# Two attention branches of a hybrid decoder kernel: probabilities divided before their transpose, outputs formed feature-major in column halves, and a new job order

## The chip, the cores and the metric

One Trainium2 chip, one core. The metric is the device time of one execution in microseconds; lower is better. The kernel was run three times before the change, and one further execution was profiled. All times below are microseconds (us) unless marked ns.

The engines are named as the profile names them: PE is TensorE (matrix products and transposes), PEld its weight loads, DVE is VectorE, ACT is ScalarE, POOL is GpSimd, and SPq is the queue of SyncE, which issues every DMA of this kernel in program order.

## The reference, cut to what matters

Two layers over a sequence of 512 tokens of width 1024. Each layer normalises x, projects it once to 9668 columns, runs five branches on parts of these columns, projects every branch output back to 1024 channels under a sigmoid gate, sums the five, applies an output projection, normalises and adds to x. The change touches two of the branches:

```python
def dsa_branch(c, pos):          # sparse attention, 4 heads x 64
    ...                          # a relu indexer picks up to 128 keys per query
    logits = jnp.einsum('bqhd,bqnhd->bhqn', qb, k_sel) * HEAD_DIM ** -0.5
    p = jax.nn.softmax(jnp.where(valid, logits, -1e30), -1)
    out = jnp.einsum('bhqn,bqnhd->bqhd', p, v_sel)
    ...
    return out * jax.nn.silu(g.astype(jnp.float32))

def memory_branch(c, mem_kv):    # cross attention into 256 memory tokens, 4 heads x 64
    ...
    p = jax.nn.softmax(jnp.einsum('bshd,bmhd->bhsm', q, km) * HEAD_DIM ** -0.5, -1)
    o = jnp.einsum('bhsm,bmhd->bshd', p, vm).reshape(bsz, seq, XATT_W)
    return o * jax.nn.silu(g.astype(jnp.float32))

def reference(...):
    for l in range(DEPTH):       # DEPTH = 2
        cols = jnp.einsum('bsd,dn->bsn', rms_norm(x, norm_pre[l]), w_in[l])
        ...
        ys = (rwkv7_branch(...), dsa_branch(...), retention_branch(...), s5_branch(...), memory_branch(...))
        for i in range(N_BRANCH):   # merged += gate_i * (ys[i] @ w_branch[l, i])
            ...
        x = x + rms_norm(merged @ w_out[l], norm_post[l])
    return x
```

## The kernel before, in words

**Dense work.** The large products (input projection, gates, branch projections, output projection) use weights split into two parts, `wh` and `wl`. A 128x512 piece of weight is fetched into one of five `raw` buffers, ACT casts it to `wh`, DVE forms `wl = raw - wh`, and PE runs three products for every 128 contraction rows (`mm3`). Each such piece of work is a `Job`. Jobs carry needs (flags of things that must be ready), and the strings `ORDER[0]` and `ORDER[1]` give the priority of the jobs in each layer: `select` takes the first one in the list whose needs are met and whose buffers fit. The letters are projections (`rsg`, `w`, `xq`, ...), and `g0` to `g4` are the gate and branch-projection jobs of the five branches: 0 is RWKV, 1 is the sparse attention, 2 retention, 3 S5, 4 cross attention. A gate job of branch b needs the branch output `y{l}{b}`.

**Branches.** Each branch is a generator (`Lane`) that yields after each step. `run` interleaves lanes with the dense work while the instructions are written out. It keeps its own estimate of each engine's clock (`Sched`); a lane's next step is written when its inputs should be ready at the PE's clock, except when DVE or ACT is more than `LAG` ahead of PE. The engines then execute their queues strictly in that written order. `LANES` gives the priority of the lanes, and `idx>4` means that lane `idx` waits for `y{l}4`. At most six lanes are active. The lane `tab` builds the tables of the S5 branch, on POOL mostly; all gate jobs of a layer need it.

**The two attention branches.** `branch_x` handles 128 queries at a time in four blocks. Scores of heads are formed in row halves of the array (`score_pair`: 64 contraction rows each, two heads side by side). DVE takes the maxima, ACT the exponentials `pr` with their sums `dn`, DVE the reciprocal. PE transposes the probabilities, ACT copies them to `xpT`, and PE forms

```python
T.matmul(po[:, h, :], pT[p][:, j, m, :], vm[:, m, 64 * h:64 * h + 64], start=m == 0, stop=m == 1)
```

so the stationary operand is 128x128 probabilities and 64 value columns move past it. The output has tokens on partitions. DVE multiplies by `1/dn` while it evicts to `xon`, and after the fourth block `to_fm` transposes the whole output back to features on partitions (eight transposes per branch and layer). `branch_dsa` does the same with causal blocks of 128 to 512 keys: one product per head and key block, `pv_(h - 1)` written behind the transposes of head h. Its tiles are `dsc` (scores, then probabilities), `dpT`, `dv` (values) and `don`.

**The seam between layers.** `finish_out` adds the normalised output of one 128-token tile to x and at once goes on to `put_hT`, which takes the squares on ACT (`xn<-x`), the scale, and the transposes into the next layer's `hh` and `hl`. The first jobs of every layer are `rq` and `rk` on halves of the tokens, so that they can start when the first two tiles are done.

Of the kernel before, what the change touches and what calls it, by code (L numbers as in the profile page):

```python
# [20 lines left out]
S = 512  # L21
# [13 lines left out]
LAG = 11.5  # L35
# [4 lines left out]
ORDER = ("rsg rv w wg g0 xq xsg di su dsg ssg dq g4 g2 dk mem1 dv g3 mem g1",  # L40
         "xsg dq g0 w di rsg wg g4 su dsg ssg dk dv g3 g1 g2")
LANES = ("ret idx>4 s5>4 ms1>3 rwkv dsa ms0 tab x>2", "idx>4 dsa>0 tab ret x rwkv>t s5")
# [40 lines left out]
class Sched:  # L83
# [5 lines left out]
    def __init__(self):  # L89
# [6 lines left out]
        self.last = (128, False, True)  # L96
# [24 lines left out]
    def matmul(self, t, ready, name, lhs, rhs):  # L121
# [11 lines left out]
        lk, lmove, lr = self.last  # L133
        if (lk, lmove) != (k, move) and self.share == 1.0:
            t += 0.085 if r and (lmove or not lr) else 0.09 if lk != k else 0.0
        self.last = (k, move, r)
# [86 lines left out]
def hybrid_kernel(ctx: ExitStack, tc: tile.TileContext, x, mem, positions, norm_pre, norm_post, norm_mem, w_in,  # L223
# [57 lines left out]
    x0 = [load_x(0, 0)]  # L281
    ncst = COFF["qdec"][0]
# [5 lines left out]
    npre = {0: bcast_row(norm_pre[0], "npre")}  # L288
# [492 lines left out]

    def rope_swap(raw, n):
# [89 lines left out]
    def branch_x(l):  # L872
# [5 lines left out]
        on = sb("xon", [128, 4, 256])  # L878
        for i in range(4):
# [14 lines left out]
            V.reciprocal(dn, dn)  # L894
            yield
# [10 lines left out]
            po = psb((128, 4, 64))  # L906
            for p in range(2):
                for j in range(2):
                    h = 2 * j + p
                    for m in range(2):  # L910
                        T.matmul(po[:, h, :], pT[p][:, j, m, :], vm[:, m, 64 * h:64 * h + 64],
                                 start=m == 0, stop=m == 1)
            V.tensor_tensor(on[:, i, :].rearrange("t (j p e) -> t j p e", j=2, p=2),
                            po.rearrange("t (j p) e -> t j p e", p=2),
                            dn.rearrange("t (p j) -> t j p", p=2)[:, :, :, None].to_broadcast([128, 2, 2, 64]),
                            op=OP.mult)
# [4 lines left out]
        for j in range(2):  # L921
            ps = to_fm(on, j)
            V.tensor_tensor(ys[l, 4][:, j, :], ps, sg[:, j, :], op=OP.mult)
            yield
# [119 lines left out]
    def branch_dsa(l):  # L1044
# [11 lines left out]
        on = sb("don", [128, 4, 256])  # L1056
        for i in range(4):
# [16 lines left out]
            V.reciprocal(dn, dn)  # L1074
            yield
            po = psb((128, 4, 64))
            pTs = []

            def pv_(h):
# [3 lines left out]
            for h in range(4):  # L1083
# [6 lines left out]
                if h:  # L1090
                    pv_(h - 1)
# [338 lines left out]
    def s5_tables(l):  # L1430
# [41 lines left out]
        for r_, w in enumerate((s5_b_re, s5_b_im)):  # L1472
            bv = w[l].rearrange("(b q) p c -> q p b c", q=2)
            for q in range(2):
                SY.dma_start(Bt[64 * q:64 * q + 64, r_], bv[q])
# [518 lines left out]
```

## Time and profile before

| | |
|---|---|
| median of three runs | 1432.06 us (1430.72 to 1433.5) |
| the profiled execution: its time | 1431.76 us |
| the profiled execution: span from first to last instruction | 1430.0 us |
| PE busy | 1373.7 us (96%) |
| DVE busy | 950.2 us (66%) |
| ACT busy | 558.3 us (39%) |
| POOL busy | 279.1 us (20%) |
| mean granted TensorE clock | 0.986 |

The time of an execution is the span plus 1.8 us around it. Busy shares are of the span. A matrix product in fp32 appears as two records in the trace, a transpose as one; the durations of single PE records overlap, so the spacing of their starts is what they cost.

### The profile page before, as it was taken

The page shows a single profiled execution, that of the slowest core. Times are in us where ns is not written, and L with a number is a line of the kernel's source. Part 1 is how long each engine was busy: PE and PEld are TensorE (multiplying, and loading weights), DVE is VectorE, ACT ScalarE, POOL GpSimd, SP SyncE. Part 2 cuts the span into 40 slices and gives each one's busy share as a digit, 9 for nine tenths or more (in the row PEclk, how much of TensorE's full clock was granted, in tenths as well). Part 3 has the DMA queues.
Part 4 walks back from the last instruction along what each step waited for, and adds up shares of the span by engine and source line. Part 5 has one row for each costly group of instructions (what it writes and reads, how often), then busy time and mean ns, then how long its engine had stood idle before and what let it go on. Part 6 is the DMA issues. An engine that isn't in the chain of part 4 may idle for free.

```text
span 1430.0 us, 21718 instructions
## 1 busy us (share of the span) xinstructions
PE 1373.7 (96%) x7774; PEld 1147.8 (80%) x7774; DVE 950.2 (66%) x2027; ACT 558.3 (39%) x1196; POOL 279.1 (20%) x329
## 2 busy tenths in 40 slices
PE   5999999999999999999979899999999999999997
PEld 5878777788878887888979788687888788778887
DVE  5677565978867864444666567668788786844465
ACT  5433445333334235233554452443323332344353
POOL 0194241000111111110019523210010112411000
PEclk9999899999999999999999899999999999999999
DMA  6644425364242432344656624263534322422355
GB/s 193 176 114 127 122 89 141 89 184 126 72 121 74 129 101 52 89 118 125 188 152 177 180 78 134 60 143 94 141 103 147 89 67 72 114 67 81 99 163 181
DMA packets 243414, 170.60 MB, mean 119 GB/s; under 512 B 27657, under 2 KB 228331, under 8 KB 243307
## 3 DMA queue, kind: packets, MB, share of 16 engines
q1 hardware_dynamic: 243307, 169.22, 42.6%
q8 instruction: 61, 1.00, 0.3%
q14 instruction: 46, 0.38, 0.1%
HBM read 144.53 MB, written 18.87 MB: 114 GB/s over the span
## 4 chain that ended last, share of the span: by engine, by line
PE 82%; DVE 6%; POOL 4%; DMA 3%; ACT 2%; issue 2%; SPq 1%; POOLq 0%; DVEq 0%; ACTq 0%
PE d L209 62%; PE b L209 19%; DVE wl L209 2%; POOL sar L209 2%; DMA raw<-in_w_out_dram 1%; POOL sta L209 1%; DMA raw<-in_w_in_dram 1%; DVE x L209 1%; SPq L209 1%; ACT wh L209 0%; DMA posi<-in_positions_dram 0%; DMA x<-in_x_dram 0%; DMA rsw<-rq 0%; POOL sem L209 0%; POOL rsw L209 0%
## 5 line engine op out<-in xcount | busy, mean ns | idle before, releaser
L209 PE MATMUL d<-hh,wh 128*128 128x512 f32 (+2 forms) x1232 | 488.3, 396 | 13.5 <-ACT wh L209 13.5
L209 PE MATMUL d<-hh,wl 128*128 128x512 f32 (+2 forms) x1232 | 474.3, 385 | 6.6 <-DVE wl L209 6.5
L209 PE MATMUL d<-hl,wh 128*128 128x512 f32 (+2 forms) x1232 | 472.1, 383 | 0.0
L209 DVE TENSOR_TENSOR wl<-raw,wh 128x512 fp32r<-128x512 f32 x448 | 334.0, 761 | 139.2 <-ACT wh L209 135.6
L209 ACT CAST wh<-raw 128x512 fp32r<-128x512 f32 x448 | 268.7, 617 | 165.6 <-PE d L209 111.9
L209 PEld LDWEIGHTS d<-hh,wh 128*128 128x128 f32 (+1 forms) x1232 | 235.6, 191 | 73.1 <-issue 15.0
L209 PEld LDWEIGHTS d<-hh,wl 128*128 128x128 f32 (+1 forms) x1232 | 234.8, 191 | 58.4 <-DVE wl L209 10.1
L209 PEld LDWEIGHTS d<-hl,wh 128*128 128x128 f32 (+1 forms) x1232 | 235.8, 191 | 42.3 <-issue 0.5
L209 POOL TENSOR_TENSOR mg<-mg,gth 128x512 f32<-128x512 f32 x48 | 69.9, 1457 | 486.2 <-DVE gth L209 486.2
L209 DVE SCALAR_TENSOR_TENSOR gth<-gth,d 128x512 f32<-128x512 f32 x64 | 43.9, 686 | 107.2 <-PE d L209 103.4
L209 ACT ACTIVATE gth<-d 128x512 f32<-128x512 f32 (+1 forms) x90 | 51.9, 577 | 159.7 <-PE d L209 155.0
L209 PE MATMUL b<-wh,mgs 128*128 128x256 f32 x320 | 63.2, 283 | 5.6 <-ACT wh L209 4.1
L209 PE MATMUL d<-yl,wh 128*128 128x512 f32 x160 | 62.9, 393 | 0.7 <-DVE yl L209 0.7
L209 PE MATMUL d<-yh,wl 128*128 128x512 f32 x160 | 62.8, 393 | 0.0
L209 PE MATMUL d<-yh,wh 128*128 128x512 f32 x160 | 62.7, 392 | 0.0
L209 PEld LDWEIGHTS b<-wh,mgs 128*128 128x128 f32 x320 | 52.1, 190 | 6.3 <-ACT wh L209 4.3
L209 DVE MAX8 dm<-dac 128x8 f32<-128x256 f32 (+2 forms) x96 | 52.8, 550 | 0.1
L209 DVE MATCH_REPLACE8 dac<-dm,dac 128x256 f32<-128x256 f32 (+2 forms) x96 | 52.1, 543 | 0.0
L209 PE MATMUL b<-wl,mgs 128*128 128x256 f32 x160 | 45.5, 285 | 0.3 <-DVE wl L209 0.3
L209 POOL TENSOR_TENSOR ors<-ors,mhalf 128x1 f32<-128x1 f32 x8 | 5.0, 634 | 203.3 <-DVE ors L209 203.3
L209 PE MATMUL d<-wh,mgs 128*128 128x256 f32 x192 | 40.6, 285 | 2.0 <-DVE ou L209 2.0
L209 POOL TENSOR_TENSOR rsw<-rsw,sinT 128x1024 f32<-128x1024 f32 (+1 forms) x12 | 29.7, 2480 | 44.0 <-DMA rsw<-diq 20.7
(399 smaller groups left out, 2067.9 us busy)
## 6 DMA issues: line engine op xcount, KB each, us to landing
raw<-in_w_in_dram SPq DMA_DIRECT2D x324, 256.0 KB, 3.4
raw<-in_w_out_dram SPq DMA_DIRECT2D x64, 256.0 KB, 4.7
raw<-in_w_branch_dram SPq DMA_DIRECT2D x40, 256.0 KB, 3.2
x<-in_x_dram SPq DMA_DIRECT2D x8, 512.0 KB, 6.0
raw<-in_w_mem_kv_dram SPq DMA_DIRECT2D x16, 256.0 KB, 2.9
s5tab<-sar SPq DMA_DIRECT2D x8, 256.0 KB, 2.0
s5Wi<-sar SPq DMA_DIRECT2D x4, 512.0 KB
nn<-wNt SPq DMA_DIRECT2D x8, 256.0 KB
```

What stands on the lines that cost most here:

```text
L209: r = f(*args, **kw)
```

## The change

Four things change.

1. In both attention branches the probabilities are multiplied by `1/dn` on DVE before they are transposed. The products swap operands: the stationary operand is now 64 value columns, the transposed probabilities move (128 columns), and two heads are written into the two column halves of the array by a new helper, `value_pair`. The outputs land with features on partitions, ACT copies them to `on`, and `to_fm` with its eight transposes per branch and layer is gone. In the sparse attention the first pair of heads is multiplied behind the transposes of the third head, the second pair after a yield.
2. `ORDER`, `LANES` and `LAG` have new values, and the planner's PE model counts a change of the array's column part as well.
3. At the start the load of `npre` comes ahead of the constants and of the second x tile, and the first weights are split before the transposes of the second x tile.
4. Three places get a `yield`: behind the stores of the S5 tables, before each load of `sBt`, and between the addition to x and `put_hT` in `finish_out`.

```diff
-LAG = 11.5
+LAG = 10.5
-ORDER = ("rsg rv w wg g0 xq xsg di su dsg ssg dq g4 g2 dk mem1 dv g3 mem g1",
-         "xsg dq g0 w di rsg wg g4 su dsg ssg dk dv g3 g1 g2")
-LANES = ("ret idx>4 s5>4 ms1>3 rwkv dsa ms0 tab x>2", "idx>4 dsa>0 tab ret x rwkv>t s5")
+ORDER = ("xq rsg rv w g1 wg g3 xsg dsg di ssg su g4 dk dq dv mem1 mem g2 g0",
+         "w xsg g1 dq di rsg dv g0 ssg su g3 g4 wg dk g2 dsg")
+LANES = ("ms1>3 tab ms0 s5 dsa>2 ret x rwkv idx>4", "ret s5>2 rwkv>4 x tab dsa>0 idx>2")
...
     x0 = [load_x(0, 0)]
+    npre = {0: bcast_row(norm_pre[0], "npre")}
...
     x0.append(load_x(0, 1))
-    npre = {0: bcast_row(norm_pre[0], "npre")}
...
+    def value_pair(out, v, pT, first, last):
+
+        sched.share = 0.5
+        for p in range(2):
+            T.matmul(out[halves[p]], v[:, halves[p]], pT(p), start=first, stop=last, skip_group_check=True)
+        sched.share = 1.0
...
# branch_x
-        on = sb("xon", [128, 4, 256])
+        on = sb("xon", [128, 2, S])
...
             V.reciprocal(dn, dn)
+            V.tensor_tensor(pr, pr, dn[:, :, None].to_broadcast([128, 4, NMEM]), op=OP.mult)
...
-            po = psb((128, 4, 64))
-            for p in range(2):
-                for j in range(2):
-                    h = 2 * j + p
-                    for m in range(2):
-                        T.matmul(po[:, h, :], pT[p][:, j, m, :], vm[:, m, 64 * h:64 * h + 64],
-                                 start=m == 0, stop=m == 1)
-            V.tensor_tensor(on[:, i, :]..., po..., dn..., op=OP.mult)
+            po = psb((128, 2, 128))
+            for j in range(2):
+                for m in range(2):
+                    value_pair(po[:, j, :], vm[:, m, 128 * j:128 * j + 128], lambda p: pT[p][:, j, m, :],
+                               m == 0, m == 1)
+            A.copy(on[:, :, ts], po)
...
         for j in range(2):
-            ps = to_fm(on, j)
-            V.tensor_tensor(ys[l, 4][:, j, :], ps, sg[:, j, :], op=OP.mult)
-            yield
+            V.tensor_tensor(ys[l, 4][:, j, :], on[:, j, :], sg[:, j, :], op=OP.mult)
+        yield
...
# branch_dsa
             V.reciprocal(dn, dn)
-            yield
-            po = psb((128, 4, 64))
+            for h in range(4):
+                V.tensor_scalar(sc[h], sc[h], dn[:, h:h + 1], None, op0=OP.mult)
+            yield
+            po = psb((128, 2, 128))
...
-            def pv_(h):
+            def pv_(j):
                 for m in range(i + 1):
-                    T.matmul(po[:, h, :], pTs[h][:, 128 * m:128 * m + 128], v[:, m, 64 * h:64 * h + 64],
-                             start=m == 0, stop=m == i)
+                    value_pair(po[:, j, :], v[:, m, 128 * j:128 * j + 128],
+                               lambda p: pTs[2 * j + p][:, 128 * m:128 * m + 128], m == 0, m == i)
...
-                if h:
-                    pv_(h - 1)
+                if h == 2:
+                    pv_(0)
             yield
-            pv_(3)
-            V.tensor_tensor(on[:, i, :]..., po, dn..., op=OP.mult)
+            pv_(1)
+            A.copy(on[:, :, ts], po)
...
# s5_tables
                 SY.dma_start(s5d["tab"][2 * l + b][:, r_], ...)
+            yield
...
             for q in range(2):
+                yield
                 SY.dma_start(Bt[64 * q:64 * q + 64, r_], bv[q])
...
# finish_out
         if l < L - 1:
+            yield
             yield from put_hT(l + 1, i, xi)
...
# first_h
-        yield from put_hT(0, i, x0[i])
+        for n, _ in enumerate(put_hT(0, i, x0[i])):
+            if n == 1 and i == 1:
+                prefetch(0, 0)
+            yield
```

## Rows read from the trace of the kernel before

**Rows 1.** The page, busy time, share of the span and instructions.

```profile
PE 1373.7 (96%) x7774; PEld 1147.8 (80%) x7774; DVE 950.2 (66%) x2027; ACT 558.3 (39%) x1196; POOL 279.1 (20%) x329
```

**Rows 2.** Stretches of 50 us: length, busy PE, PEld, DVE, ACT, POOL, clock, DMA, GB/s.

```profile
0.00:50.00 50.00, 33.52 (x221) 31.69 (x222) 30.21 (x70) 25.45 (x47) 2.51 (x10) 0.93 0.63 180
...
300.00:350.00 50.00, 50.00 (x293) 40.86 (x292) 40.34 (x101) 16.58 (x36) 1.62 (x2) 1.00 0.44 126
...
700.00:750.00 50.00, 41.14 (x330) 40.34 (x330) 33.79 (x70) 26.54 (x64) 5.59 (x12) 0.97 0.60 179
750.00:800.00 50.00, 41.42 (x311) 40.78 (x311) 26.94 (x34) 20.56 (x43) 38.41 (x78) 0.86 0.68 189
...
1400.00:1430.00 30.00, 20.41 (x171) 19.98 (x169) 16.54 (x33) 9.57 (x23) 2.69 (x4) 0.94 0.49 164
```

**Rows 3.** The waits of PE, whole run: us in total, times, longest.

```profile
PE d L209 <- ACT wh L209: 13.5, 4, 8.4
...
PE b L209 <- ACT wh L209: 4.1, 1, 4.1
...
PE b L209 <- ACT dpT L209: 1.9, 8, 0.2
```

**Rows 4.** Group of PE instructions by form: records, busy us, mean ns.

```profile
L209 PE MATMUL b<-dv,dpT 128*128 128x64 f32 x160 | 22.5, 272 | 2.2 <-ACT dpT L209 1.9
```

**Rows 5.** Timeline, one block's value products of cross attention: start, us, what.

```profile
191.14 1.97 PEld L209 LDWEIGHTS b<-xvm,xpT 128*128 128x128 f32 x16
...
191.36 1.89 PE L209 MATMUL b<-xvm,xpT 128*128 128x64 f32 x16
```

**Rows 6.** Timeline of PE around one block's scores in row halves.

```profile
523.60 0.39 PE L209 MATMUL d<-hl,wh 128*128 128x512 f32 x1
523.83 0.40 PE L209 MATMUL d<-hh,wl 128*128 128x512 f32 x1
524.16 0.71 PE L209 MATMUL b<-dk,dq 64*128 64x128 f32 x8
...
525.14 0.39 PE L209 MATMUL d<-hl,wh 128*128 128x512 f32 x1
```

**Rows 7.** Timeline of PE from value products of sparse attention back to dense.

```profile
544.39 0.66 PE L209 MATMUL b<-dv,dpT 128*128 128x64 f32 x4
...
545.17 0.39 PE L209 MATMUL d<-hl,wh 128*128 128x512 f32 x1
```

**Rows 8.** Timeline of PE around four transposes of `to_fm`.

```profile
237.08 0.60 PE L209 MATMUL b<-cst,xon 128*128 128x128 f32 x4
...
237.75 0.39 PE L209 MATMUL d<-hl,wh 128*128 128x512 f32 x1
```

**Rows 9.** Groups of DVE instructions by form: busy, mean ns, idle before them.

```profile
L209 DVE TENSOR_TENSOR xon<-b,xdn 128x256 f32<-128x256 f32 x8 | 3.4, 419 | 6.2 <-PE b L209 6.1
...
L209 DVE TENSOR_TENSOR diq<-diq,cosT 128x1024 f32<-128x1024 f32 x2 | 2.4, 1210 | 0.0
...
L209 DVE TENSOR_SCALAR wta<-wta,hka,oka 128x512 f32<-128x512 f32 x4 | 2.2, 545 | 0.1
```

**Rows 10.** Timeline of DVE at the start of the run.

```profile
9.11 2.74 DVE L209 SCALAR_TENSOR_TENSOR xn<-x,xrs,npre 128x512 f32<-128x512 f32 x4
```

**Rows 11.** Timeline of ACT at the seam between the layers.

```profile
717.44 1.06 ACT L209 ACTIVATE xn<-x 128x1024 f32<-128x1024 f32 x1 [1.54 <-DVE x L209]
...
718.49 2.16 ACT L209 CAST wh<-raw 128x512 fp32r<-128x512 f32 x4
```

**Rows 12.** Timeline of PE 30 us later at the seam; idle time before in brackets.

```profile
749.73 0.39 PE L209 MATMUL d<-hh,wh 128*128 128x256 f32 x1 [2.99 <-ACT wh L209]
```

**Rows 13.** Timeline of the DMA queue at the S5 tables of layer 1.

```profile
779.86 5.05 SPq L209 DMA_DIRECT2D s5tab<-sar  x4
...
787.81 2.66 SPq L209 DMA_DIRECT2D raw<-in_w_in_dram  x5
```

**Rows 14.** Timeline of ACT where the last gate of layer 1 begins.

```profile
1317.69 0.62 ACT L209 CAST yh<-ys 128x512 fp32r<-128x512 f32 x1 [0.20 <-PE d L209]
```

More of the change, by code (lines that the diff above doesn't have):

```diff
@@ L95, in __init__ @@
         self.landing = [0.0] * 8
-        self.last = (128, False, True)
+        self.last = ((True, True), False, True)
         self.window, self.activity, self.half = 8.0, 0.0, True
@@ L132, in matmul @@
         t = max(t, ready)
[L133 to L136, printed above, removed]
+        part = (k > 64, c > 64)
+        last, lmove, lr = self.last
+        if (last, lmove) != (part, move) and self.share == 1.0:
+            t += 0.085 if r and (lmove or not lr) else 0.09 if last != part else 0.0
+        self.last = (part, move, r)
         self.turn(t)
@@ L905, in branch_x @@
             yield
-            po = psb((128, 4, 64))
-            for p in range(2):
-                for j in range(2):
-                    h = 2 * j + p
-                    for m in range(2):
-                        T.matmul(po[:, h, :], pT[p][:, j, m, :], vm[:, m, 64 * h:64 * h + 64],
-                                 start=m == 0, stop=m == 1)
[L913 to L916, printed above, removed]
+            po = psb((128, 2, 128))
[4 more added lines that the diff above has]
+            A.copy(on[:, :, ts], po)
         resize(f"y{l}4", c4=3)
@@ L1055, in branch_dsa @@
         v = ST[l, "dv"]
-        on = sb("don", [128, 4, 256])
+        on = sb("don", [128, 2, S])
         for i in range(4):
@@ L1089, in branch_dsa @@
                 pTs.append(pT)
-                if h:
-                    pv_(h - 1)
+                if h == 2:
+                    pv_(0)
             yield
-            pv_(3)
-            V.tensor_tensor(on[:, i, :].rearrange("t (h e) -> t h e", h=4), po,
-                            dn[:, :, None].to_broadcast([128, 4, 64]), op=OP.mult)
+            pv_(1)
+            A.copy(on[:, :, ts], po)
         resize(f"y{l}1", c4=3)
@@ L1100, in branch_dsa @@
         for j in range(2):
-            ps = to_fm(on, j)
-            V.tensor_tensor(ys[l, 1][:, j, :], ps, sg[:, j, :], op=OP.mult)
-            yield
+            V.tensor_tensor(ys[l, 1][:, j, :], on[:, j, :], sg[:, j, :], op=OP.mult)
+        yield
     def wsb(name, shape, dt=F32, bufs=2):
```

## The prediction

> **What bounds the kernel now.** I read the page's busy shares first: PE is busy for 1373.7 of 1430.0 us, so 56.3 us are idle in all [rows 1]. Then I asked for busy time in stretches of 50 us, because a share over the whole run hides where the idle time lies. It lies in three places [rows 2]: the first 50 us (16.5 idle), the seam between the layers from 700 to 800 us (8.9 and 8.6), and the last 30 us (9.6). Those make 43.5 us; the other 1250 us hold only 12.8. In the middle, as from 300 to 350 us, PE is busy all the time while DVE has 9.7 of 50 us free. So in the middle of a layer a us of PE work saved is a us of run time, as long as the lanes deliver their branch outputs in time; at the ends the time goes by what PE waits for. The waits of PE name these: `wh`, the cast weights, leads with 13.5 and 4.1 us, all at the seam, and the probabilities of the sparse attention cost only 1.9 us in eight waits [rows 3].
>
> **The change part by part.** The sum is made against the profiled execution: 1430.0 us of span and 1.8 around it make 1431.8, which is 0.3 below the median of the three runs. A change of 0.2% (2.9 us) is about what the three runs can tell from none.
>
> *Value products.* The code has 64 of them in the cross attention (2 layers, 4 blocks, 4 heads, 2 key blocks) and 80 in the sparse one, and the trace shows two records for each, 160 for the sparse one [rows 4] and 16 in each of the eight blocks of the cross attention [rows 5]. Sixteen take 1.89 us; less the 0.27 us tail of the last one that is 15 steps of 0.108 us [rows 5]. The count stays at 288 after the change, but each now streams 128 columns past 64 stationary ones. No row shows column halves. The bounds: four transposes, which stream 128 columns, take 0.67 us together with one dense record of 0.23, so 0.11 each [rows 8]; without any sharing nothing is gained. The nearest row with two products side by side is the score pair, also fp32 and also 128 moving columns: eight records in 0.71 us, less a tail of 0.30, are 7 steps of 0.059 [rows 6]. It is nearest in data type, columns and pairing, so I take 0.059: 288 x 0.049 = 14.1 us gained (0 to 15.6, the latter at half of 0.108).
>
> The Trainium skill's page "TensorEngine Tiling (Array Packing)", section "Overview" ("Theoretical Speedup"), gives up to twice the throughput when the stationary operand has at most 64 columns; by it alone this term would be 15.6, and no run here shows it yet.
>
> *Transposes.* `to_fm` goes from both branches: 8 transposes x 2 branches x 2 layers = 32, at 0.11 us [rows 8], 3.5 us gained. They enter and leave at no visible cost.
>
> *Changing the array's shape.* From a dense record to a score pair it takes 0.33 us instead of 0.23, so 0.10 to enter; from the pair to the second dense record behind it 0.98 us, less 8 x 0.059 and 0.23, so 0.28 to leave [rows 6]. Leaving the present value products costs 0.78 - 4 x 0.108 - 0.23 = 0.12 [rows 7]. The new code enters column halves 8 times in the cross attention and 16 in the sparse one: 24 x (0.10 + 0.28 - 0.12) = 6.2 us lost (0 if the halves of columns need no change of shape, 9.1 if nothing is to be deducted).
>
> *The copies of probabilities.* PE now waits once per block for the copy of head h while it has the transposes of head h+1 to do [rows 3]. Later it does three heads' transposes and then needs the copies of two. The copies run on ACT one behind the other, so the one wait gets longer by part of a copy; I take 0.25 us x 8 = 2 us lost (0 to 4).
>
> *Vector work.* The division adds 8 multiplies of 128x1024, 1.21 us each, and 32 of up to 128x512, at most 0.545 each: 9.7 and at most 17.4 us. Sixteen evictions of 0.42 us leave DVE for ACT [rows 9], where a copy of the same size should cost about the same. DVE gains at most 20 us on its 950, and ACT 7 on 558. I cost it at nothing, because the dense products of PE run beside it and DVE has 9.7 of 50 us free in a full stretch of the middle [rows 2]. Without that cover each block's chain from reciprocal to transpose would be 1.2 to 2.2 us longer, at most 27 us over 16 blocks. The new ACT copy waits for PE, as the DVE eviction does now (6.1 us in 8 cases in the cross attention [rows 9]). Behind it in ACT's queue stand casts of `wh`, and PE waits for those; but two pieces of weight are kept split ahead of PE, some 5.6 us of dense work in the middle of a layer (24 records at 0.23), and such a wait is 0.8 us. Again nothing.
>
> *The start.* DVE begins to scale the first x tile at 9.11 us, when `npre` has landed as the fourth load [rows 10]. Second in the queue, `npre` comes two loads earlier and the first tile is scaled early, but the second x tile now lands last and has squares and scale still before it. I see 1.2 us (0 to 2).
>
> *The yields.* At the seam the squares of two tiles stand in ACT's queue ahead of the cast of `wh` and wait for DVE's addition to x; the cast starts at 718.49 [rows 11], and PE stands for 4.1 us behind it; the same pattern 30 us later costs 3.0 [rows 12]. Another 8.4 us is the longest wait of the run for `wh` [rows 3]. With a yield between the addition and the squares, casts can be written in between. That longest wait comes from the DMA queue: the stores of the S5 tables sit at its head from 779.86 us until POOL has finished, four `sBt` loads follow, and the next weights go out at 787.81 [rows 13]. The yield there can take only the `sBt` part away, 2.9 us (779.86 + 5.05 to 787.81). Together 4.1 + 3.0 + 2.9 = 10 us at the most; since weights must still arrive and POOL is as late as ever, I take half, 5 us (0 to 10).
>
> *The order.* No row shows it. The middle stretches leave it 12.8 us to gain at best. I put it at zero; what it may lose is a rival.
>
> Sum: 1431.8 - 14.1 - 3.5 + 6.2 + 2 - 1.2 - 5 = 1416.2 us. All bounds on the good side give 1431.8 - 15.6 - 3.5 - 2 - 10 = 1400.7, on the bad side 1431.8 - 3.5 + 9.1 + 4 = 1441.4.
>
> **The rivals.**
>
> *The halves do not share the array.* Then the value products keep 0.108 us and the changes of shape are still paid: 1416.2 + 14.1 = 1430.3, no change. For it speaks that the two moving streams come from the same 128 partitions, unlike those of a score pair; against it, that a dense record passes 512 columns in 0.23 us, 0.45 ns each [rows 6], while a transpose needs 0.11 us for 128, 0.86 ns each [rows 8]: the moving side can deliver fp32 words at twice the rate at which such a record takes them.
>
> *Weight loads of one half do not run beside products of the other.* A record would pay 0.054 us for 64 weight columns (half of the 0.108 that 128 take now) and 0.11 for the stream, 0.164 in place of 0.059: 288 x 0.105 = 30.2 us lost, 1446.4. Rows speak against it: the 16 loads of a block take 1.97 us and its 16 products 1.89, over the same time and the same 128 rows [rows 5]. The Trainium skill's page "TensorE: Matmul & The Clock Gate", section "Part 3: Packing small matmuls — row/col tiling", says that a weight load overlaps products in flight only where their row groups differ, which would bring this about; the trace does not agree, with 0.108 us a record where load and stream in turn would take longer.
>
> *The sparse attention of layer 1 comes late.* This one is slower. Its output is cast at 1317.69 us, when the fourth gate's products are just done [rows 14], so PE has no other work left: the chain RWKV, then sparse attention, already ends on the beat. If PE saves time ahead of it and the chain does not move, the gain is lost to waiting; if the new order, in which RWKV waits for the cross attention in layer 1, makes it later, the run is longer by as much. The run ends 1431.8 - 1317.7 = 114.1 us after that cast, so it is slower than before from the point at which the cast comes after 1317.7. A chain that is late by 20 us at RWKV and by at most 8.7 at four blocks of division (4 heads x 0.545 x 4), less 15 that the PE saves ahead of it, gives 1445.5. Against it: `w` now stands first in layer 1, ahead of `xsg` and `dq`, so RWKV gets its inputs four tiles (some 22 us at 24 records of 0.23) sooner.
>
> *The order also closes gaps.* All of the yields and half of the middle gaps: 1416.2 - 5 - 6.4 = 1404.8.
>
> **How the numbers follow.** Forecast 0.58 (its own range 1409 to 1424), order closes gaps 0.14, halves do not share 0.11, loads do not overlap 0.03, late chain 0.14. The likeliest gives 1416.2. The range runs from 1401, the good bounds, to 1438, which leaves out the worst of the two slower rivals, some 2 in 10 with what may lie below 1401. Faster by over 0.2%: 0.58 + 0.14 and half of the 0.11, 0.77. Within 0.2%: 0.07, most of it from halves that do not share. Slower: 0.16.
>
> **What would show it.** In the profile after: value products with 64 stationary columns in steps of about 0.06 us; if 0.11, the halves do not share. The group of `to_fm` transposes of `xon` and `don` gone. The first dense record behind a value pair 0.2 to 0.3 us late. No ACT square between two casts of `wh` at the seam while PE waits; the wait of 8.4 us down to about 6. The last gate's cast of layer 1 some 15 us before 1317.7, with no PE idle ahead of it. The prediction is wrong if PE idle time in the middle grows beyond 12.8 us, which would be the order, or if the seam keeps its 17.5 us.

## The result and the profile after

The changed kernel takes 1415.04 us (median; 1413.4 to 1415.91) beside 1431.39 for the kernel before on the same chip: ratio 0.9889 (95% interval 0.9862 to 0.9917), 15.9 us faster by that ratio. The forecast was 1416.2. The profiled execution took 1413.4 with a span of 1411.6, again 1.8 around it. Line L209 of before is L210 here.

The page of the changed kernel, busy time [rows 1]:

```profile
PE 1357.6 (96%) x7742; PEld 1123.6 (80%) x7742; DVE 960.2 (68%) x2046; ACT 562.0 (40%) x1212; POOL 290.0 (21%) x334
```

PE is busy 16.1 us less, and its idle time is 54.0 us in place of 56.3. It lies elsewhere, as the stretches of the changed kernel show (columns as in [rows 2]):

```profile
0.00:50.00 50.00, 35.02 (x240) 32.71 (x241) 31.55 (x70) 26.88 (x50) 3.01 (x10) 0.97 0.69 191
150.00:200.00 50.00, 43.48 (x246) 35.30 (x245) 30.96 (x66) 26.66 (x68) 18.17 (x14) 0.86 0.39 119
200.00:250.00 50.00, 43.68 (x263) 32.99 (x262) 29.02 (x47) 21.96 (x59) 7.48 (x8) 0.93 0.35 88
...
700.00:750.00 50.00, 44.62 (x368) 43.57 (x367) 37.98 (x81) 29.36 (x70) 14.74 (x29) 1.00 0.67 198
750.00:800.00 50.00, 48.27 (x353) 45.39 (x352) 32.04 (x41) 24.83 (x52) 30.96 (x53) 0.97 0.84 221
```

The same view of the kernel before, for the two stretches that were not shown:

```profile
150.00:200.00 50.00, 47.45 (x243) 36.98 (x241) 31.69 (x65) 23.67 (x58) 12.30 (x9) 0.90 0.36 106
200.00:250.00 50.00, 49.33 (x278) 39.36 (x279) 27.13 (x54) 27.58 (x72) 14.09 (x13) 0.97 0.47 130
```

The seam went from 17.4 to 7.1 us idle, and its clock from 0.97 and 0.86 to 1.00 and 0.97. From 150 to 250 us, where the cross attention of layer 0 runs beside the preparation of RWKV, a hole opened: 12.8 us idle where there were 3.2, and a lower clock. The waits of PE in the changed kernel, whole run [rows 3]:

```profile
PE d L210 <- DVE wl L210: 12.6, 15, 1.6
...
PE b L210 <- DVE wrks L210: 3.7, 1, 3.7
PE d L210 <- ACT wh L210: 2.8, 2, 1.5
...
PE b L210 <- ACT dpT L210: 0.5, 1, 0.5
```

Cast weights `wh` cost 17.6 us before and cost 4.1 now (2.8 and one of 1.3). Waits for `wl`, which VectorE makes, cost 13.6 us now (12.6 and one of 1.0) where they cost 7.6. The value products by form, and one pair of the sparse attention among dense records on PE's timeline, both of the changed kernel [rows 4, 7]:

```profile
L210 PE MATMUL b<-dpT,dv 128*64 128x128 f32 x160 | 14.5, 285 | 0.8 <-ACT dpT L210 0.5
L210 PE MATMUL b<-xpT,xvm 128*64 128x128 f32 x128 | 9.4, 285 | 0.3 <-ACT xpT L210 0.3
```

```profile
1296.79 0.39 PE L210 MATMUL d<-hh,wl 128*128 128x512 f32 x1
1297.11 1.09 PE L210 MATMUL b<-dpT,dv 128*64 128x128 f32 x16
1298.13 0.50 PE L210 MATMUL d<-hh,wh 128*128 128x512 f32 x1
1298.47 0.39 PE L210 MATMUL d<-hl,wh 128*128 128x512 f32 x1
```

Sixteen records in 1.09 us, less the tail of 0.27, are 15 steps of 0.055 on the average (0.108 before). Entering takes 0.32 instead of 0.23, so 0.09; leaving 1.36 - 16 x 0.055 - 0.23 = 0.25.

The next table splits the profiled execution of each kernel, which can lie some us off the median beside it, into three stretches. The marks are the first record of each layer's output projection (its other operand is `mgs`) on PE's timeline. The seam lies in the middle stretch. The kernels e1 to e12 are told of below.

| kernel | median us | ratio to before (95%) | start to projection 0 | projection 0 to 1 | from there to the end of the span |
|---|---|---|---|---|---|
| before | 1431.39 | | 682.7 | 691.0 | 56.3 |
| changed | 1415.04 | 0.9889 (0.9862, 0.9917) | 683.5 | 671.9 | 56.2 |
| e8, yields alone | 1420.81 | 0.9946 (0.9924, 0.9967) | 684.3 | 679.0 | 56.3 |
| e3, all but the attention | 1414.83 | 0.9902 (0.9878, 0.9925) | 678.8 | 675.6 | 59.3 |
| e9, cross attention old | 1405.57 | 0.9840 (0.9818, 0.9862) | 676.0 | 671.9 | 55.9 |
| e11, sparse attention old | 1428.41 | 0.9992 (0.9974, 1.0010) | 688.3 | 683.4 | 55.7 |
| e2, attention alone | 1433.79 | 1.0040 (1.0021, 1.0059) | 681.0 | 693.7 | 55.5 |
| e5, no yields | 1429.12 | 0.9998 (0.9987, 1.0010) | 681.6 | 688.5 | 55.7 |
| e4, old order | 1417.43 | 0.9915 (0.9895, 0.9936) | 681.7 | 678.9 | 56.0 |
| e1, halves in turn | 1417.56 | 0.9912 (0.9893, 0.9931) | 684.5 | 674.0 | 57.8 |
| e6, no division | 1398.95 | 0.9793 (0.9774, 0.9812) | 673.9 | 670.1 | 55.8 |
| e7, wide products | 1421.97 | 0.9945 (0.9929, 0.9962) | 688.6 | 677.6 | 55.8 |
| e10, division on ScalarE | 1415.15 | 0.9905 (0.9886, 0.9924) | 680.3 | 677.0 | 55.7 |
| e12, division in two steps | 1414.04 | 0.9891 (0.9869, 0.9912) | 680.3 | 677.1 | 55.9 |

Differences between kernels below are those of ratios times 1430 us. The interval of a single ratio is 1.6 to 3.9 us to either side, widest for the changed kernel, so a difference of two kernels is uncertain by 4 to 5 us.

### The profile page after: what moved, and what is told of

Same layout as the page of the kernel before. It is cut to its first block, busy times and chain, and to the rows that moved or that the text cites. A ratio compares the mean times of both kernels' runs of the same rounds, so it can differ in the third digit from the quotient of the medians.

```text
span 1411.6 us, 21674 instructions
## 1 busy us (share of the span) xinstructions
PE 1357.6 (96%) x7742; PEld 1123.6 (80%) x7742; DVE 960.2 (68%) x2046; ACT 562.0 (40%) x1212; POOL 290.0 (21%) x334
## 4 chain that ended last, share of the span: by engine, by line
PE 79%; DVE 9%; DMA 3%; ACT 3%; issue 3%; POOL 3%; SPq 1%; DVEq 0%; POOLq 0%; ACTq 0%
PE d L210 62%; PE b L210 18%; DVE wl L210 2%; DMA raw<-in_w_out_dram 1%; POOL sar L210 1%; DVE xmx L210 1%; ACT xp L210 1%; ACT wh L210 1%; SPq L210 1%; DMA raw<-in_w_in_dram 0%; DMA posi<-in_positions_dram 0%; POOL sta L210 0%; DMA x<-in_x_dram 0%; DVE ys L210 0%; DVE ml L210 0%
## 5 line engine op out<-in xcount | busy, mean ns | idle before, releaser
L210 PE MATMUL d<-hh,wh 128*128 128x512 f32 (+2 forms) x1232 | 484.2, 393 | 1.5 <-ACT wh L210 1.5
L210 PE MATMUL d<-hh,wl 128*128 128x512 f32 (+2 forms) x1232 | 472.2, 383 | 10.8 <-DVE wl L210 10.6
L210 PE MATMUL d<-hl,wh 128*128 128x512 f32 (+2 forms) x1232 | 469.7, 381 | 0.0
L210 DVE TENSOR_TENSOR wl<-raw,wh 128x512 fp32r<-128x512 f32 x448 | 336.0, 762 | 128.6 <-ACT wh L210 126.0
L210 ACT CAST wh<-raw 128x512 fp32r<-128x512 f32 x448 | 268.5, 617 | 118.7 <-PE d L210 76.2
L210 PEld LDWEIGHTS d<-hh,wl 128*128 128x128 f32 (+1 forms) x1232 | 232.6, 189 | 64.5 <-DVE wl L210 16.7
L210 PEld LDWEIGHTS d<-hh,wh 128*128 128x128 f32 (+1 forms) x1232 | 233.3, 189 | 60.7 <-issue 13.4
L210 PEld LDWEIGHTS d<-hl,wh 128*128 128x128 f32 (+1 forms) x1232 | 233.4, 189 | 42.5 <-issue 0.2
L210 POOL TENSOR_TENSOR mg<-mg,gth 128x512 f32<-128x512 f32 x48 | 68.3, 1423 | 474.1 <-DVE gth L210 474.1
L210 ACT ACTIVATE gth<-d 128x512 f32<-128x512 f32 (+1 forms) x90 | 52.1, 579 | 173.2 <-PE d L210 173.1
L210 DVE SCALAR_TENSOR_TENSOR gth<-gth,d 128x512 f32<-128x512 f32 x64 | 43.9, 686 | 92.7 <-PE d L210 91.6
L210 PE MATMUL b<-wh,mgs 128*128 128x256 f32 x320 | 62.6, 281 | 1.5 <-DVE ou L210 1.5
L210 PE MATMUL d<-yh,wl 128*128 128x512 f32 x160 | 62.9, 393 | 0.0
L210 PE MATMUL d<-yl,wh 128*128 128x512 f32 x160 | 62.7, 392 | 0.0
L210 PE MATMUL d<-yh,wh 128*128 128x512 f32 x160 | 62.7, 392 | 0.0
L210 PEld LDWEIGHTS b<-wh,mgs 128*128 128x128 f32 x320 | 51.4, 188 | 2.0 <-DVE ou L210 1.9
L210 DVE MAX8 dm<-dac 128x8 f32<-128x256 f32 (+2 forms) x96 | 52.8, 550 | 0.0
L210 DVE MATCH_REPLACE8 dac<-dm,dac 128x256 f32<-128x256 f32 (+2 forms) x96 | 52.1, 542 | 0.0
L210 POOL TENSOR_TENSOR ors<-ors,mhalf 128x1 f32<-128x1 f32 x8 | 5.0, 635 | 208.5 <-DVE ors L210 208.5
L210 PE MATMUL b<-wl,mgs 128*128 128x256 f32 x160 | 45.1, 282 | 1.2 <-DVE wl L210 1.0
L210 PE MATMUL d<-wh,mgs 128*128 128x256 f32 x192 | 40.3, 282 | 2.7 <-DVE ou L210 2.7
L210 POOL TENSOR_TENSOR rsw<-rsw,sinT 128x1024 f32<-128x1024 f32 (+1 forms) x12 | 28.7, 2402 | 47.6 <-DMA rsw<-diq 23.0
```

Of the source, the lines that this page charges most:

```text
L210: r = f(*args, **kw)
```

## The experiments

**e1: the two column halves one after the other.** The changed kernel in the same written order, save that all products of one half come before those of the other.

```diff
-    for m in range(n):
-        for p in range(2): T.matmul(out[halves[p]], v(m)[:, halves[p]], pT(p, m), ...)
+    for p in range(2):
+        for m in range(n): T.matmul(out[halves[p]], v(m)[:, halves[p]], pT(p, m), ...)
```

> The changed kernel with the same instructions in the same places, but within each group of value products all those of the first column half come before all those of the second; the planner is told the old sequence, so its plan stays. If two halves run side by side and products in one half follow each other at 0.109 us a record, a block of the cross attention takes 13 steps of 0.109 in place of 8, and the four blocks of the sparse attention 1, 3, 5 and 7 steps more per pair of heads: 8 x 0.55 + 32 x 0.109 x 2 = 11.4 us in all, some 1426 us, if every us of PE counts. Rival: the time of the changed kernel does not come from halves side by side, and this stays within 3 us of 1415.

3.3 us slower: far from 1426, within the 3 us of the rival, and not clear of the noise. So the run's time decides nothing here, and the records have to. PE's timeline of this kernel, a cross attention's sixteen (in runs of four) and a sparse one's (in runs of eight); L791 is the line of these products in it:

```profile
840.03 1.14 PE L791 MATMUL b<-xpT,xvm 128*64 128x128 f32 x16
...
1299.85 1.58 PE L791 MATMUL b<-dpT,dv 128*64 128x128 f32 x16
```

With halves alternating (two records of one half, then two of the other, since a product is two records) both take 1.09. So runs of four lose almost nothing, and runs of eight lose 0.49; runs of six, twelve records, take 1.14 here and 0.88 there.

The starts of the single records show why. In the changed kernel the sixteen at 1297.11 start in eight pairs, one record of each half, 0.007 us apart, and the pairs follow each other every 0.109 us. In e1 the first half's eight records from 1299.85 on are 0.109 apart as well (in both the first step is 0.16), and the other half's first starts 0.006 us behind the fifth of them. So a record in one half takes 0.11 us, and the other half runs beside it except for what stands more than four records ahead of it. It gives (8 - 4 + 8) x 0.11 + 0.27 = 1.59 and (6 - 4 + 6) x 0.11 + 0.27 = 1.15. The rival's reason is out, since the halves do run side by side. My expectation of 0.108 for every record left out that they overlap in longer runs too. All blocks together lose 8 x 0.05 + 4 x 0.26 + 4 x 0.49 = 3.4 us of PE; PE's busy time rose by 2.7.

**e7: all 128 value columns loaded.** The other side of the same question; the outputs of the two heads are mixed in this kernel.

```diff
-    T.matmul(out[halves[p]], v[:, halves[p]], pT(p), ...)
+    T.matmul(out, v, pT(p), ...)
```

> The changed kernel with each value product loading all 128 value columns of its pair and writing all 128 output rows (so that the outputs of two heads are mixed); count, moving columns and written order stay. Theory, the weight load sets the price of a value product, and the change gained by halving it, not by two halves that run side by side: a record takes 0.108 us again in place of 0.055, PE's busy time rises by 12 to 16 us less some 0.3 for each of 24 changes of shape that are gone, and the run takes 1418 to 1424 us where the products lie in the path, 1414 to 1417 where they fill waits. Rival, the 128 moving columns set it: 0.055 to 0.06 a record, and the run takes 1406 to 1412 us, since the changes of shape are gone.

PE's timeline of this kernel, the pair that answers to the one at 1297.11:

```profile
1307.26 1.95 PE L788 MATMUL b<-dpT,dv 128*128 128x128 f32 x16
1308.96 0.48 PE L210 MATMUL d<-hh,wh 128*128 128x512 f32 x1
```

(1.95 - 0.27) / 15 = 0.112 a record, PE busy 1371.2, 8.0 us slower than the changed kernel. So 128 columns cost what they cost before. In e1, 64 columns in one half take 0.11 too; so it is not the number of weight columns that halves the price but the other half beside it. The theory that I gave to this run had the right number for a reason that e1 does not bear out.

**e2 and e3: the two sides apart.** e2 is the kernel before with the new attention code and the planner's column model; e3 is the changed kernel with the attention of before, without that column model.

> The kernel before with the new attention code and the planner's model of the array's column part; order, lanes, LAG, start and yields as before. If the attention code saves PE time by its own rows (15.4 value products, 3.5 transposes, less 6 of changing shape), some 13 us: 1418 us (1415 to 1423). Rival: the gain is the order's and the yields', and this stays above 1427.

> The kernel before with the new order, lanes, LAG, start and yields, and the old attention code. If seam and start gain 12 to 15 us and the order loses some 8 between 150 and 250 us: 1424 to 1428 us. Rival that the schedule is neutral: 1431. Rival that the hole between 150 and 250 us is the division's and not the order's: about 1418.

Both fell out against me: e2 lies where its rival said, and e3 below 1424, near its second rival. The attention alone is 0.4% slower: PE is busy 12.2 us less and idle 12.3 us more. Order, start and yields alone give all that the change gives.

**e4, e5, e8: order and yields.** e4 puts the old `ORDER`, `LANES` and `LAG` into the changed kernel; e5 takes its three yields out; e8 is the kernel before with them.

```diff
# e8, and the reverse in e5
         for r_ in range(2):
             ...                  # stores of the S5 tables
+            yield
...
+                yield
                 SY.dma_start(Bt[64 * q:64 * q + 64, r_], bv[q])
...
+            yield
             yield from put_hT(l + 1, i, xi)
```

> The changed kernel with the old order, lanes and LAG. If the yields gave the seam its gain and the new order made the hole between 150 and 250 us: 1407 to 1411 us. Rival that the new order gave the seam its gain, by finishing the S5 tables earlier: 1417 to 1422 us, with the wait of 8 us for weights back in the trace.

> The changed kernel without its three yields (behind the stores of the S5 tables, before each load of sBt, between the addition to x and put_hT); order, attention and start stay. Theory, the yields free the seam: PE's idle time from 700 to 800 us goes from 7 us back to 14 to 18, a wait of several us for a cast wh stands there again behind the S5 table stores, and the run takes 1421 to 1426 us. Rival, the new order has POOL done earlier at the seam and that alone empties it: 700 to 800 us stays under 10 us idle, and the run takes 1414 to 1418.

> The kernel before with the three yields alone: old order, old attention, old start. Theory, the yields are worth what the chain of waits at the seam showed: idle time from 700 to 800 us falls from 17.4 us to 8 to 12, and the run takes 1421 to 1426 us. Rival, they need the new order, since POOL finishes the tables as late as ever: 15 us or more idle there, and the run takes 1428 to 1432 us.

The yields are worth 7.7 us alone, with 8.0 us idle from 700 to 800 us, and without them the changed kernel gains nothing: it has 15.8 us idle there, and its waits of PE are those of before (11.3 in two and 4.1 in one). From 700 to 800 us in e5:

```profile
PE d L210 <- ACT wh L210: 11.3, 2, 8.3
PE b L210 <- ACT wh L210: 3.2, 1, 3.2
```

The three yields were not tried one by one, so how the gain divides among them is not shown. With the old order (e4) the changed kernel is 3.7 us slower, which is not clear of the noise. That time lies in the rival's range, but not for its reason: the seam is idle for 7.7 us only and no wait of 8 us for weights is back. Nor did the new order make the hole, since 9.0 us are idle from 150 to 250 us without it. Why the yields give more than a cast's place in ACT's queue is seen on POOL. POOL's timeline before (idle ahead of an instruction in brackets), and then in e8:

```profile
742.05 0.20 POOL L209 COPY sem<-un 128x16 f32<-128x16 f32 x1
746.75 0.98 POOL L209 TENSOR_TENSOR xrs<-xrs,mhalf 128x1 f32<-128x1 f32 x1 [4.50 <-DVE xrs L209]
749.44 0.55 POOL L209 TENSOR_TENSOR xrs<-xrs,mhalf 128x1 f32<-128x1 f32 x1 [1.71 <-DVE xrs L209]
749.95 0.52 POOL L209 TENSOR_TENSOR sar<-sar,sem 128x8 f32<-128x8 f32 x1
```

```profile
738.23 0.20 POOL L209 COPY sem<-un 128x16 f32<-128x16 f32 x1
738.50 0.21 POOL L209 TENSOR_TENSOR sar<-sar,sem 128x8 f32<-128x8 f32 x1
...
744.28 1.49 POOL L209 TENSOR_TENSOR xrs<-xrs,mhalf 128x1 f32<-128x1 f32 x2
745.74 0.21 POOL L209 TENSOR_TENSOR sar<-sar,sem 128x16 f32<-128x16 f32 x1
```

Before, POOL's queue held the root `xrs` of two tiles, which waits for their squares, ahead of the S5 tables, and the tables stood 7.7 us behind the copy. With the yield the first steps of the tables are written ahead of the roots and run while the squares are made. So the tables are done sooner and the stores, in two pairs, leave the DMA queue early. The queue in the changed kernel [rows 13]:

```profile
772.45 1.13 SPq L210 DMA_DIRECT2D s5tab<-sar  x2
773.68 1.01 SPq L210 DMA_DIRECT2D raw<-in_w_in_dram  x2
776.70 0.81 SPq L210 DMA_DIRECT2D s5tab<-sar  x2
777.61 1.49 SPq L210 DMA_DIRECT2D raw<-in_w_in_dram  x3
779.15 0.69 SPq L210 DMA_DIRECT2D sBt<-in_s_b_re_dram  x1
```

In e8 they go at 772.15 and 775.95, and in e5, without the yields, all four go from 778.32 on in one piece, so this is the yields' doing. On ACT the casts now stand between the squares; ACT's timeline of the changed kernel [rows 11]:

```profile
715.12 1.06 ACT L210 ACTIVATE xn<-x 128x1024 f32<-128x1024 f32 x1 [0.62 <-DVE x L210]
...
716.17 0.60 ACT L210 CAST wh<-raw 128x512 fp32r<-128x512 f32 x1
716.68 1.05 ACT L210 ACTIVATE xn<-x 128x1024 f32<-128x1024 f32 x1
```

**e6: the division left out, the written order unchanged.**

```diff
-    V.tensor_tensor(pr, pr, dn[:, :, None].to_broadcast([128, 4, NMEM]), op=OP.mult)
...
-        V.tensor_scalar(sc[h], sc[h], dn[:, h:h + 1], None, op0=OP.mult)
```

> The changed kernel without the multiplication of the probabilities by 1/dn in both branches (the output lacks the division by the sums); every other instruction is in the same order. Theory, the division is exposed in the cross attention, since the transposes of the probabilities come behind it and the dense work written beside it is too short: the idle time of PE from 150 to 250 us falls from 12.8 us to 5 to 9, from 800 to 850 us by 1 to 2, and the run takes 1405 to 1411 us. Rival, the hole at 150 to 250 us is one of the order of work and the division lies under other work: the idle time there stays within 2 us of 12.8, and the run takes 1413 to 1416.

13.7 us faster than the changed kernel, more than the theory asked. The end of a cross attention block of layer 0 on DVE's timeline in the changed kernel, and the PE instruction that follows it:

```profile
221.59 0.17 DVE L210 TENSOR_SCALAR xmx<-xmx 128x2 f32<-128x2 f32 x1
223.61 0.18 DVE L210 RECIPROCAL xdn<-xdn 128x4 f32<-128x4 f32 x1 [1.86 <-ACT xp L210]
223.82 1.22 DVE L210 TENSOR_TENSOR xp<-xp,xdn 128x1024 f32<-128x1024 f32 x1
224.97 0.17 DVE L210 COPY wrks<-b 128x16 f32<-128x16 f32 x1
```

```profile
225.19 1.94 PE L210 MATMUL b<-cst,xp 128*128 128x128 f32 x8 [3.71 <-DVE wrks L210]
```

The wait is put down to `wrks`, the last to end; what PE needs is `xp`, divided just ahead of it. In e6 the first four of these transposes start ahead of both the reciprocal and `wrks`:

```profile
217.38 0.66 PE L210 MATMUL b<-cst,xp 128*128 128x128 f32 x4
```

```profile
218.26 0.18 DVE L210 RECIPROCAL xdn<-xdn 128x4 f32<-128x4 f32 x1 [1.81 <-ACT xp L210]
218.36 0.14 DVE L210 COPY wrks<-b 128x16 f32<-128x16 f32 x1
```

There they start 0.15 us behind the exponentials of the first two heads, in the changed kernel 2.62 us behind them: with the division they wait for all four heads, the reciprocal and the multiply, which is more than the 1.2 us of the multiply alone.

From block to block the reciprocals are 1.3 to 1.6 us closer, and the gating of the output comes at 223.69 instead of 232.80: 9.1 us, of which 1.2 were there before the first division. PE's 3.7 us wait is gone, idle time from 150 to 250 us is 6.5 in place of 12.8, and the granted clock 0.90 and 1.00 in place of 0.86 and 0.93. PE's 7742 records stand in the same order in e6 and in the changed kernel, so the lead of e6 can be read record by record. The lead is 1.2 us before the first division, 9.1 at 250 us and still at 500, 9.6 after the sparse attention of layer 0, 7.9 after the seam, 11.3 after the cross attention of layer 1, and 11.4 after the sparse attention of that layer. So in these executions the cross attention's eight divisions cost some 11 us (7.9 and 3.4) and the sparse attention's 32 cost 0.6, since those lie under other work.

From 150 to 250 us the lead grows where PE waits in the changed kernel: 1.11 us (at 190.49) and 1.59 (at 206.24) for `wl`, and the 3.71 for the fourth block. The first of these `wl` stands just behind a division in VectorE's queue (the division from 187.57 to 189.42, `wl` at 189.34).

**e9, e11: one branch old.** Each is the changed kernel with one branch's hunks taken back. With e3 and the changed kernel they make four corners.

> The changed kernel with the cross attention of before (division at the eviction, 128 stationary probabilities, transposes of the output), and all else as changed. Theory, VectorE sets the pace of the stretch in which the cross attention runs beside the preparation of RWKV (180 to 230 us), and each division there is paid in full: idle time of PE from 150 to 250 us falls from 12.8 to 6 to 8 us, some 7 us of PE work come back, and the run takes 1407 to 1413 us, faster than the changed kernel by 2 to 7. Rival, the cross attention's new form pays for its division by the PE time it saves: 1413 to 1417.

> The changed kernel with the sparse attention of before and the cross attention as changed; the fourth corner beside both old (1414.8), cross attention old (1405.6) and both new (about 1414.5). Theory, the two branches add up: the new sparse attention is worth 9 us because its divisions lie under other work and its PE time is saved, the new cross attention costs 9 us, so this corner takes 1421 to 1426 us, with the first product of layer 0's output projection 3 to 6 us later than in the changed kernel. Rival, the 9 us come from how the written order falls out for one kernel and not from the branches: the corner takes 1412 to 1418.

Both go somewhat further than their theories: e9 is faster than 1407 us and e11 slower than 1426, with the first projection 4.8 us later than in the changed kernel, as expected. The new sparse attention gains 8.9 us with the old cross attention beside it (e3 to e9) and 14.7 with the new one (e11 to changed). The new cross attention loses 7.0 and 12.9. So the signs are settled; that the sizes hang on each other, by 6 us, is within the uncertainty of four ratios. e9 is faster than both kernels. Its stretches from 150 to 250 us:

```profile
150.00:200.00 50.00, 42.58 (x260) 34.94 (x259) 29.91 (x70) 26.76 (x68) 17.38 (x14) 0.97 0.39 118
200.00:250.00 50.00, 48.72 (x287) 38.24 (x286) 29.53 (x51) 24.48 (x62) 12.13 (x10) 1.00 0.48 120
```

PE starts or ends 547 records there, where it is 509 in the changed kernel. The profiled executions differ by 7.8 us, and 7.5 of them are won before the first projection; from there on the two are alike.

**e10, e12: the division elsewhere.**

```diff
# e10
-    V.tensor_tensor(pr, pr, dn..., op=OP.mult)
+    for u in range(4):
+        A.activation(pr[:, u, :], pr[:, u, :], AF.Copy, scale=dn[:, u:u + 1])
# e12
+    for p in range(2):
+        V.reciprocal(du, du)             # two heads of dn
+        V.tensor_tensor(pu, pu, du..., op=OP.mult)
```

> The changed kernel with the cross attention's division made by ScalarE, four multiplies of 128x256 by a scale for each block, in place of the one multiply of 128x1024 on VectorE. Theory, VectorE's queue is what the division holds up: VectorE is relieved of 12 us, ScalarE has 27 of 50 us free in 180 to 230 us, and the run takes 1404 to 1410 us. Rival, the chain from scores to transposes is what counts and it is no shorter (four multiplies of some 0.35 us on ScalarE): 1412 to 1417.

> The changed kernel with the cross attention's reciprocal and division in two steps, one for each two heads, so that the first can run while ScalarE still forms the exponentials of the other two (VectorE stands for 1.3 to 1.9 us ahead of the reciprocal in the changed kernel). Theory, most of the first half disappears in that gap: some 0.6 us a block on VectorE and on the chain, and where VectorE sets the pace the idle time of PE shrinks: 1408 to 1412 us. Rival, the chain is covered by other work and nothing changes: 1413 to 1417.

Neither beats the changed kernel. Up to 796.7 us PE's records stand in the same order in e10, e12 and the changed kernel, so these can be compared record by record too. Both are 3.1 us ahead from 250 us on, of which 1.3 (e10) and 1.8 (e12) were there before the first division; e6 is 9.1 ahead, 1.2 of them from before. So taking the division out of VectorE's queue gives back 2 of some 8 us, and VectorE's queue alone is not what makes the division dear. How much of the rest is the longer chain and how much, in e10, the place of the division in ScalarE's queue is not shown.

At the seam both lose the lead, to one wait for `wh` that the changed kernel does not have, 3.49 us in e10 and 3.42 in e12. PE's timeline of e10:

```profile
774.56 0.39 PE L210 MATMUL d<-hh,wh 128*128 128x256 f32 x1 [3.49 <-ACT wh L210]
```

In both the DMA queue holds 253 loads of weights ahead of the S5 stores of layer 1 and in the changed kernel 254, so one weight more goes out behind the stores, which wait for POOL. Behind 796.7 us the written order differs, and what that adds is not taken apart.

## Why the total was right and its parts were not

Three of the runs lead from the kernel before to the changed one step by step. This sets their steps against the sum that was forecast:

| part | forecast us | measured us |
|---|---|---|
| yields (before to e8) | -5 | -7.7 |
| order and start (e8 to e3) | -1.2 | -6.3 |
| sparse attention (e3 to e9) | -7.8 - 1.8 + 4.2 + 2 = -3.4 | -8.9 |
| cross attention (e9 to changed) | -6.3 - 1.8 + 2.1 = -6.0 | +7.0 |
| all | -15.6 | -15.9 |

Each measured step is uncertain by 3 to 5 us, and the sizes hold for this way through the runs alone: without the yields everything else together gains nothing (e5), so at the end of the way the yields are worth 15.6 us.

**Work, clock and idle time.** PE's busy time is its work and what a lower clock adds to it. In these traces the granted clock is 1.0 or 0.5 of full speed (2.4 or 1.2 GHz), and eight transposes that take 1.04 us at 1.0 (at 214.81) take 1.94 at 0.5 (at 225.19). So the two can be parted by weighing every stretch of busy time with its clock. The sums of three kernels with the same PE records (before, e3, e8) agree within 3 us. In us, of the profiled executions:

| kernel | work at full clock | added at half clock | idle | span |
|---|---|---|---|---|
| before | 1357.9 | 15.8 | 56.3 | 1430.0 |
| e8, yields alone | 1359.9 | 8.8 | 50.9 | 1419.6 |
| e3, all but the attention | 1356.8 | 8.2 | 48.6 | 1413.6 |
| e9, cross attention old | 1350.6 | 6.8 | 46.4 | 1403.8 |
| changed | 1345.6 | 12.0 | 54.0 | 1411.6 |
| e6, no division | 1346.2 | 8.2 | 45.4 | 1399.8 |

So the forecast of PE's own work was good: 14.1 + 3.5 - 6.2 = 11.4 us less, and it fell by 12.3. What I left out is the clock. Before, it is 0.5 in three stretches of the seam, from 719.6, 750.3 and 787.8 us on, two just behind and one inside PE's three waits for `wh` there; in e8 it is 1.0 throughout the seam. From e9 to the changed kernel the work falls by 5.0, but idle time grows by 7.6 and the part at half clock by 5.2. One of its stretches, from 222.8 us on, begins inside the wait of 3.71 us, and e6 has none there; others begin ahead of the first division, so not all of the 5.2 is shown to be the division's.

**Value products, right.** 0.055 us in place of 0.108, so 15.4 us of PE where I had 14.1. The two rivals on the array are out: the halves share it, and in each half a weight load of 0.137 us starts every 0.109, while products run. The Trainium skill's page "TensorEngine Tiling (Array Packing)", section "Overview", gives up to twice the speed for at most 64 stationary columns; the trace agrees, with 0.108 to 0.055. The Trainium skill's page "TensorE: Matmul & The Clock Gate", section "Part 3: Packing small matmuls — row/col tiling", has loads overlap products only where row groups differ; the trace does not agree, with these loads and products on the same 128 rows.

**Shape and copies.** Entering and leaving cost 0.34, so 24 x (0.34 - 0.12) = 5.3 (forecast 6.2). The copies gained instead of losing: one wait of 0.5 us for `dpT` where eight made 1.9 [rows 3]; forecast was +2. With these the sparse attention's PE side comes to 160 x -0.053 - 1.8 + 16 x 0.22 - 1.4 = -8.2, near the -8.9 that was measured. `to_fm` is gone as forecast.

**Vector work, the step that failed.** "I cost it at nothing, because the dense products of PE run beside it and DVE has 9.7 of 50 us free in a full stretch of the middle." The cross attention's PE side is 128 x -0.053 - 1.8 + 8 x 0.22 = -6.8; measured is +7.0, so some 13.8 us were lost, and e6 gives 13.7 back without the divisions. With 5 us of uncertainty on each, that they agree so closely is luck. It lies within the 27 that I wrote for no cover, though by another sum: in the sparse attention the cover held, and in the cross attention the chain grew by more than the multiply. I looked for cover in the stretch from 300 to 350 us, where no attention runs. From 180 to 230, where it does, DVE is busy 37.9 of 50 us after the change (28.6 before) and of its 12.1 free us 5.6 stand just ahead of the four reciprocals, in wait for the exponentials of the same block (1.15, 1.27, 1.27, 1.86): free time that the division cannot use. The stretch before, and then in the changed kernel:

```profile
180.00:230.00 50.00, 48.54 (x293) 38.28 (x292) 28.63 (x55) 26.04 (x80) 17.30 (x16) 0.97 0.35 106
```

```profile
180.00:230.00 50.00, 43.24 (x254) 32.57 (x254) 37.94 (x57) 22.60 (x61) 20.05 (x15) 0.88 0.19 51
```

That "PE idle time in the middle grows beyond 12.8 us" was my own sign of a wrong prediction, and it did, to 22.8 (54.0 less 15.0, 7.1 and the last 30 us' 9.1). I wrote that this would be the order; it is the attention, since e3 with the new order has 15.7 and e2 with the old one 25.5.

**The yields and the order, too small.** That "POOL is as late as ever" was wrong: POOL's lateness was itself a wait behind the roots, and the yield lifted it. In e8 the seam's idle time falls by 9.4 us, nearly all of the 10 that I had as the most, and the clock there rises. (The waits for `wh` were not "all at the seam": 15.4 of the 17.6 us were.) I put the order at zero because "no row shows it", so this side was forecast at 6.2 and gave 14.0. The rival in which the order also closes gaps has 11.4 more, 17.6, and is nearer, but not for its reason: in e3 the middle is idle for 15.7 us, not for less than the 12.8 of before. Why the order gains is open. That the total came out is luck: two errors of 8 us with opposite signs.

**The start and the end.** The first dense record starts at 14.36 instead of 15.32, near the 1.2, and at 14.46 to 15.01 in the other runs with this start. But DVE scales the first tile later (9.69 for 9.11), not earlier, so it did not come about as I wrote. The late chain of layer 1 did not come: the last gate's first cast is 15.3 us earlier [rows 14]. ACT's timeline of the changed kernel:

```profile
1302.38 1.22 ACT L210 CAST yh<-ys 128x512 fp32r<-128x512 f32 x2 [1.45 <-DVE ys L210]
```

## What to carry to other kernels

Ask for cover in the stretch where the added instruction will stand, and whether the engine's free time there comes before or after the thing it must wait for: a mean over another stretch says nothing. An instruction that waits at the head of one engine's queue holds back everything written behind it, so look at the queue of the least busy engine too when a table or a store is late. Try the parts of a change apart and together before believing a total: here the fastest kernel that still divides (e9) takes only half of the attention's change. Where two kernels have the same records in the same order, compare them record by record: the lead shows where the time goes.

## What the hardware showed that was not expected

- A multiply of 128x1024 on DVE takes 1.23 us alone, and 1.85 and 3.15 in the two of eight cases in which an instruction of POOL had begun before it. One that began 0.66 us ahead of POOL's multiply kept its 1.23 (at 794.33). DVE's and POOL's timelines of the changed kernel:

```profile
806.70 3.15 DVE L210 TENSOR_TENSOR xp<-xp,xdn 128x1024 f32<-128x1024 f32 x1
...
822.60 1.23 DVE L210 TENSOR_TENSOR xp<-xp,xdn 128x1024 f32<-128x1024 f32 x1
```

```profile
806.36 2.41 POOL L210 TENSOR_TENSOR rsw<-rsw,sinT 128x1024 f32<-128x1024 f32 x1 [1.05 <-DMA rsw<-rk]
```

  Over the eight blocks the division took 12.3 us, 1.54 each, where 1.21 was forecast.
- Each column half takes 0.109 us a record and the two run side by side, as long as the records of one do not stand more than four ahead of the other's in the queue: runs of four records lose 0.05 us in sixteen, runs of eight 0.49 (e1).
